# Second FFN's down product as seven half-size products, and softmax sums divided at the end of branch A

## Chip, cores and metric

One NeuronCore of a Trainium2 chip. The metric is the device time of one launch in microseconds: the median of three runs, and beside it one execution recorded by the profiler, from which all rows below come.

## Reference: what is computed

A decoder layer on 1024 tokens of width 1024 in fp32: a SwiGLU half-step, a token mixer of two causal attention branches, a second SwiGLU half-step. Each has an RMSNorm before and after. What the change touches:

```python
def swiglu(h, w_gate, w_up, w_down):                       # D_FF = 2816
    return (jax.nn.silu(h @ w_gate) * (h @ w_up)) @ w_down
...
    h = rms_norm(x, g_pre_ffn2[l]) * (1 + sc3) + sh3
    x = x + 0.5 * gt3 * rms_norm(swiglu(h, w_gate2[l], w_up2[l], w_down2[l]), g_post_ffn2[l])
...
# branch A, per block of 128 queries and each of 8 heads
    s = jnp.where(valid[:, :, None, :], s, -jnp.inf)
    p = jax.nn.softmax(s, axis=-1)
    return jnp.einsum('bqhk,bqkr->bqhr', p.astype(c_kv.dtype), ckv_sel)
```

## The kernel before

**Products.** Every large product is taken in three TensorE passes (`mm3`, L102): each fp32 operand is split into a high and a low part, high x high, low x high and high x low are summed in one PSUM bank. A split is one ScalarE cast (L76) and one VectorE subtraction (L77) of a 128x512 tile; `psplit` (L81, L82) puts the subtraction on GpSimd. The engines get their order from a planner in the framework (L1404, `schedule_with_timeline_sim=True`), so the order on an engine is not just that of the source; waits between engines are semaphores.

**Gate and up (`gate_up`, L252).** Both FFNs run gate and up already with seven half-size products in place of eight: for each of 11 blocks b of 256 hidden columns there are steps i = 0 to 6, each with 24 matmuls for gate and up (m = 0, 1). Sums of weight quarters are made by GpSimd (L286 to L289), sums of results by VectorE (L343, L346). In steps 1, 4, 5 and 6 one quarter of the activation is complete: ScalarE takes Silu (L349), GpSimd multiplies (L351), and a DMA of the SyncE queue (SP) stores the 256 KB to DRAM (L353). Step 1 gives the first token half and even hidden blocks, step 4 first half and odd, step 5 second half and odd, step 6 second half and even. The blocks b = 0 to 2 take steps 0 and 1 first ("early"). The result tile `p1` of step 1 has one buffer, `p0` three, `p2` and `p3` one each. Weights are prepared three steps ahead (LOOK, L27).

**Down (`down`, L368).** It loops three times over the 22 hidden chunks c: eight token tiles x first 512 columns, then token tiles 0 to 3 and 4 to 7 x the second 512 columns. For each chunk a 512 KB load of w_down feeds two chunks (L393), w_down and the activation are split, and each token tile gets three matmuls. The activation is read back from DRAM once (L389) into tiles that stay. Each finished bank is drained by ScalarE (sum of squares, L365) and VectorE (times the gain, L366). After the last chunk of a column half the kernel takes rsqrt of the sums and adds the residual (`post2`, L1363; DMAs L1366, L1369, L1379). In the last loop of the second FFN the last four chunks are kept back and run token tile by token tile, so that banks end one after another.

**Branch A (`branch_a`, L971).** 64 units (4 head pairs p, 2 heads e, 4 groups g, 2 blocks t). `scores`: three matmuls per 512 keys, then one VectorE instruction that masks, scales and takes the extreme (L1058), exp with the sum on ScalarE (L1061), reciprocal of the sum on VectorE (L1062), and GpSimd multiplies the probabilities with it (L1063). `mix`: TensorE transposes the probabilities (L1081), ScalarE and VectorE split them (L76, L77), TensorE multiplies with the values (L1091) after each second unit, ScalarE and VectorE add the two halves of the bank (L1095, L1097). With p = 2 each pair of units also carries a small combination of branch B (`combine_b`: VectorE on 4 to 12 elements per partition, L951 to L960; GpSimd L962 to L964).

Of the kernel before, what the change touches and what calls it, by code (L numbers as in the profile page):

```python
# [10 lines left out]
F32 = mybir.dt.float32  # L11
# [28 lines left out]
class Layer:  # L40
# [211 lines left out]
    def gate_up(self, W, raws, pools, V, wg, wu, actd):  # L252
# [64 lines left out]
        def steps(order, filler=None, ahead=()):  # L317
# [4 lines left out]
            for s, (b, i) in enumerate(order):  # L322
# [4 lines left out]
                for m in range(2):  # L327
# [19 lines left out]
                    if i in (1, 4, 5, 6):  # L347
                        if m == 0:
                            nc.scalar.activation(x[0], x[0], AF.Silu)  # L349
                        else:  # L350
                            nc.gpsimd.tensor_tensor(x[1], x[1], x[0], op=ALU.mult)  # L351
                            ff, h = {1: (0, 0), 4: (1, 0), 5: (1, 1), 6: (0, 1)}[i]
# [15 lines left out]
    def down(self, W, W2, wd, room, actd, y, G, junk, ss, post, filler=None):  # L368
# [6 lines left out]
        for dh, tiles in ((0, range(8)), (1, range(4)), (1, range(4, 8))):  # L375
# [3 lines left out]
            nlate = (1, LATE + (W2 is not None) * 2 if tiles[-1] == 7 else 1)[dh]  # L379
# [6 lines left out]
            for c in range(NF):  # L386
# [8 lines left out]
                pool = W2 if W2 is not None and nlate > 1 and NF - nlate <= c < NF - nlate + 2 else W  # L395
                w = [pool.tile([P, 512], F32R, name=f"d{n}", tag="w") for n in "hl"]
                self.split(w[0], w[1], r[:, c % 2])
                a = {}
                for h in halves:
                    a[h] = [pool.tile([P, 512], F32R, name=f"a{n}", tag="w") for n in "hl"]  # L400
# [21 lines left out]
        for _ in bg:  # L422
            pass
# [547 lines left out]
    def branch_a(self, aw, ap, late, G, mask, off):  # L971
# [73 lines left out]
        def scores(p, e, g, t):  # L1045
# [4 lines left out]
            st = late.tile([P, 2], F32, name="st", bufs=4)  # L1050
# [122 lines left out]
def layer_kernel(ctx, tc, aps, out):  # L1173
# [22 lines left out]
    with pool("w1", 12) as W, pool("g1") as wk, pool("r1", 5) as L.rawp:  # L1196
# [48 lines left out]
        with pool("f1a") as fa, pool("f1b") as fp:  # L1245
# [30 lines left out]
            L.down(W, None, aps["w_down1"], room, actd, y, A1, lambda: jkb, ss, post1, fill)  # L1276
# [31 lines left out]
    actd = L.dram.tile([DFF // P, P, S], F32, name="act2")  # L1308
    L.turns = {"pj": cycle(("pj", "s", "pj", "pt"))}
    with pool("w3", 13) as W, pool("r5", 3) as L.rawp, pool("o2") as op:  # L1310
# [36 lines left out]
        with pool("r6", 2) as r6, pool("vp2") as vp:  # L1347
# [60 lines left out]
```

## Time and profile before

| | us |
|---|---|
| median of 3 runs (lowest to highest) | 2521.93 (2517.61 to 2523.97) |
| the profiled execution, its own time | 2520.3 |
| its span in the profile | 2518.4 |
| TensorE busy (94% of the span) | 2357.4 |
| VectorE busy (64%) | 1611.1 |
| ScalarE busy (43%) | 1094.7 |
| GpSimd busy (38%) | 951.2 |
| DMA, mean over the span | 119 GB/s |
| TensorE clock granted, mean | 0.974 |

Busy shares are means over stages with different limits. Matmuls are pipelined in the records: the length of one record is not the time that it takes from the next, so TensorE's cost is read from the distance of starts. The stretches that matter are 1456 to 1646 us (branch A), 1900 to 2265 us (gate and up of the second FFN) and 2265 to 2518 us (its down product and the end).

### The profile page before, as it was taken

Reading aid. Unit: us, or ns where it says so; the run is one execution under the profiler, and the core shown is the slowest. Engines: PE = TensorE matmul, PEld = TensorE weight load, DVE = VectorE, ACT = ScalarE, POOL = GpSimd, SP = SyncE. Lnnn points to the kernel's source line nnn. Section 1 sums busy time; section 2 is a strip of 40 time slices with the busy share of each in tenths; the row PEclk is TensorE's granted clock in tenths of the full one; section 3 lists DMA queues with packets and bytes.
Section 4 is the critical chain, followed back from the end, with each engine's and each line's share of the span. In section 5 each row is a group of like instructions: output and inputs, shape, how many; then the busy total and the mean of one; then the engine's idle time right before and its main releaser. Section 6 shows DMA issues by size and latency. Waiting matters only on the chain.

```text
span 2518.4 us, 33990 instructions
## 1 busy us (share of the span) xinstructions
PE 2357.4 (94%) x11279; PEld 1978.4 (79%) x11279; DVE 1611.1 (64%) x3193; ACT 1094.7 (43%) x2342; POOL 951.2 (38%) x1109
## 2 busy tenths in 40 slices
PE   5799999999998999999989799899879999999997
PEld 4578887778787877889989677678658888888886
DVE  7866778754885145999963388874486554553455
ACT  5422322333454355777445466623443333333443
POOL 5675555400004433432243144601587454430012
PEclk9899999999998999999999799999989999999999
DMA  9234455761634233512421422154234323253134
GB/s 279 89 107 134 145 159 153 240 230 51 190 117 122 73 99 97 193 33 66 142 59 51 104 64 70 45 198 158 96 113 130 97 76 92 80 195 107 53 107 151
DMA packets 229804, 300.04 MB, mean 119 GB/s; under 512 B 23607, under 2 KB 144343, under 8 KB 229629
## 3 DMA queue, kind: packets, MB, share of 16 engines
q1 hardware_dynamic: 228988, 296.80, 37.4%
q8 instruction: 90, 1.47, 0.2%
q10 hardware_dynamic: 640, 1.07, 0.1%
q14 instruction: 86, 0.70, 0.1%
HBM read 233.98 MB, written 63.83 MB: 118 GB/s over the span
## 4 chain that ended last, share of the span: by engine, by line
PE 75%; DVE 11%; DMA 5%; issue 3%; ACT 3%; POOL 3%; SPq 0%; DVEq 0%; ACTq 0%; POOLq 0%
PE gu L104 9%; PE gu L105 9%; PE gu L106 9%; PE dn L105 6%; PE dn L106 6%; PE dn L104 6%; PE gpj L104 2%; PE gpj L105 2%; PE gpj L106 2%; PE bq L104 2%; DMA wr<-in_w_mod_dram 2%; PE bq L105 2%; PE bq L106 1%; PE apv L1091 1%; PE bv L104 1%
## 5 line engine op out<-in xcount | busy, mean ns | idle before, releaser
L104 PE MATMUL gu<-V,wh 128*128 128x512 f32 x1232 | 488.5, 397 | 18.9 <-ACT wh L76 9.3
L105 PE MATMUL gu<-V,wl 128*128 128x512 f32 x1232 | 487.3, 396 | 6.0 <-DVE wl L77 5.7
L106 PE MATMUL gu<-V,wh 128*128 128x512 f32 x1232 | 482.3, 394 | 4.5 <-DVE V L77 4.5
L77 DVE TENSOR_TENSOR wl<-rw,wh 128x512 fp32r<-128x512 f32 x232 | 214.1, 925 | 134.6 <-PE gu L105 93.7
L104 PEld LDWEIGHTS gu<-V,wh 128*128 128x128 f32 x1232 | 234.6, 191 | 73.3 <-ACT wh L76 11.3
L105 PEld LDWEIGHTS gu<-V,wl 128*128 128x128 f32 x1232 | 234.3, 190 | 59.7 <-DVE wl L77 8.9
L106 PEld LDWEIGHTS gu<-V,wh 128*128 128x128 f32 x1232 | 233.3, 190 | 56.5 <-DVE V L77 7.0
L105 PE MATMUL dn<-dh,al 128*128 128x512 f32 x704 | 275.6, 391 | 1.6 <-DVE al L77 1.6
L106 PE MATMUL dn<-dl,ah 128*128 128x512 f32 x704 | 274.4, 391 | 0.0
L104 PE MATMUL dn<-dh,ah 128*128 128x512 f32 x704 | 253.7, 391 | 6.0 <-DVE junk L197 6.0
L76 ACT CAST wh<-rw 128x512 fp32r<-128x512 f32 x232 | 140.1, 618 | 210.0 <-PE gu L106 126.3
L351 POOL TENSOR_TENSOR p<-p 128x512 f32<-128x512 f32 x86 | 129.9, 1511 | 247.3 <-DVE p L343 70.1
L343 DVE TENSOR_TENSOR p<-gu,p 128x512 f32<-128x512 f32 x252 | 170.0, 681 | 67.2 <-PE gu L106 35.6
L76 ACT CAST ah<-act 128x512 fp32r<-128x512 f32 x176 | 107.4, 621 | 182.3 <-PE dn L105 131.2
L77 DVE TENSOR_TENSOR al<-act,ah 128x512 fp32r<-128x512 f32 x176 | 118.0, 689 | 80.5 <-PE dn L105 42.5
L104 PEld LDWEIGHTS dn<-dh,ah 128*128 128x128 f32 x704 | 132.5, 188 | 33.9 <-DVE junk L197 6.4
L105 PEld LDWEIGHTS dn<-dh,al 128*128 128x128 f32 x704 | 132.7, 189 | 30.5 <-DVE al L77 3.2
L77 DVE TENSOR_TENSOR dl<-rd,dh 128x512 fp32r<-128x512 f32 x132 | 91.2, 692 | 101.4 <-PE dn L105 52.4
L106 PEld LDWEIGHTS dn<-dl,ah 128*128 128x128 f32 x704 | 132.9, 189 | 27.7
L349 ACT ACTIVATE p<-p 128x512 f32<-128x512 f32 x86 | 54.4, 633 | 215.4 <-DVE p L343 163.8
L185 DVE SCALAR_TENSOR_TENSOR macc<-wr,scol,macc 128x512 f32<-128x512 f32 x98 | 91.9, 938 | 56.0 <-DMA wr<-in_w_mod_dram 55.4
L76 ACT CAST dh<-rd 128x512 fp32r<-128x512 f32 x132 | 81.6, 618 | 83.3 <-PE dn L105 70.8
(465 smaller groups left out, 5465.4 us busy)
## 6 DMA issues: line engine op xcount, KB each, us to landing
rd<-in_w_down_dram SPq DMA_DIRECT2D x66, 512.0 KB
wr<-in_w_mod_dram SPq DMA_DIRECT2D x112, 256.0 KB
rw<-in_w_gate_dram SPq DMA_DIRECT2D x44, 512.0 KB
rw<-in_w_up_dram SPq DMA_DIRECT2D x44, 512.0 KB
act<-act SPq DMA_DIRECT2D x88, 256.0 KB
act<-p SPq DMA_DIRECT2D x86, 256.0 KB
wm<-in_w_mod_dram SPq DMA_DIRECT2D x32, 256.0 KB
x<-xt SPq DMA_DIRECT2D x16, 512.0 KB
```

The source lines that it names most:

```text
L76: self.nc.scalar.copy(hi, src)
L77: self.nc.vector.tensor_sub(lo, src, f(hi))
L104: mm(out, ah, bh, start=start, stop=False)
L105: mm(out, al, bh, start=False, stop=False)
L106: mm(out, ah, bl, start=False, stop=stop)
L185: nc.vector.scalar_tensor_tensor(acc, r, self.scol[:, k:k + 1], acc, op0=ALU.mult, op1=ALU.add)
L343: nc.vector.tensor_tensor(x[m], bk, y[m], op=ALU.add)
L349: nc.scalar.activation(x[0], x[0], AF.Silu)
L351: nc.gpsimd.tensor_tensor(x[1], x[1], x[0], op=ALU.mult)
L1091: nc.tensor.matmul(b[:, q0:256], VV[p][:, j, e, :], pt[j // 4][l][:, j % 4, q0:], start=j == 0 and l == 0, stop=j == nj - 1 and l == 1)
```

## The change

- **Down product.** `down7` replaces `down` in the second FFN (the first FFN keeps `down`, with the same loops). With the token halves and the even or odd hidden blocks as a 2x2 grid (a11, a12 second half of tokens; a21, a22 first half), and the same for w_down (b11 to b22), it takes seven products of 512 tokens x 1408 hidden x 512 columns: a11 b11, s3 (b22 - b12), s2 (b22 - b12 + b11), s1 (b12 - b11), a22 (b22 - b12 + b11 - b21), a12 b21, s4 b22, in this order.
- **Sums of w_down** are made by GpSimd just ahead of the split, for products 2 to 5, 11 chunks each; the running sum of products 2, 3 and 5 stays in two tiles `TT` and is updated in place, the sum of product 4 overwrites its load.
- **Sums of the activation** (s1 = a21 + a22, s2 = s1 - a11, s3 = a11 - a21, s4 = a12 - s2) are made in `gate_up` from the quarters while they are in SBUF: three on GpSimd, one on VectorE for each block b. Seven tiles per block go to DRAM instead of four (three early blocks also store a21 and read it back). `down7` reads one tile per chunk and product.
- **Buffers.** `down7` loads pairs of chunks: activation, w_down, and for products 2 and 4 a second part of w_down. Product 1 uses the buffers of `gate_up`; from product 2 the loads have six buffers of 512 KB (`dr2`), the splits 24 + 13 (`dw2`, `w3`). Two sets of four PSUM banks alternate. y and `TT` take the four large tiles.
- **Results** are summed in SBUF: VectorE adds each finished bank to one or two of the four quarters of y; a finished quarter gets its sum of squares (ScalarE, now from SBUF) and its gain (VectorE).
- **Branch A.** L1063 and the reciprocal per unit go. The sums of two units share a tile; after L1091 VectorE takes one reciprocal of 128x2, TensorE transposes it twice as a 128x128 broadcast into the free half of the bank, and VectorE multiplies the 64x256 result with it.

```diff
@@ gate_up
+        def operands(b, i, x):
+            out = lambda n, t: nc.sync.dma_start(ad[n, b], t)
+            sub = lambda E, o, x, y: E.tensor_tensor(o, x, y, op=ALU.subtract)
+            if i == 1:
+                tiles[b, "21"] = x
+                if b in early:
+                    out(7, x[1])
+                return
+            if i != 1:
+                tiles[b, {4: "22", 5: "12", 6: "11"}[i]] = x
+                out({4: 1, 5: 2, 6: 0}[i], x[1])
+            if i == 4:
+                if b in early:
+                    t = pools["p1"].tile([P, 2, 512], F32, name="p1", tag="p1", bufs=1)
+                    nc.sync.dma_start(t[:, 1], ad[7, b])
+                    tiles[b, "21"] = [t[:, 0], t[:, 1]]
+                nc.gpsimd.tensor_tensor(x[0], tiles[b, "21"][1], x[1], op=ALU.add)
+                out(3, x[0])
+            if i == 6:
+                (s1, _), (s3, a21), (s4, a12), (s2, a11) = (tiles[b, n] for n in ("22", "21", "12", "11"))
+                sub(nc.gpsimd, s2, s1, a11)
+                out(4, s2)
+                sub(nc.vector, s3, a11, a21)
+                out(5, s3)
+                sub(nc.gpsimd, s4, a12, s2)
+                out(6, s4)
...
+    def down7(self, Ws, raws, wd, T, ad, y, G, junk, ss, post, nlate):
...
+        tags = (("pj", "pj", "s", "pt"), ("tr", "tr", "o", "gg"))
...
+        def normed(r, c, t, E):
+            nc.scalar.activation(junk(), C(r, c, t), AF.Square, accum_out=sq(r, c, t))
+            E.tensor_tensor(C(r, c, t), C(r, c, t), G[:, dsl[c - 1]], op=ALU.mult)
...
+        def o6(b, t):
+            add(C(1, 2, t), C(1, 1, t), b)
+            add(C(2, 1, t), C(2, 1, t), b)
+
+        def o5(b, t):
+            add(C(1, 2, t), C(1, 2, t), b)
+            add(C(2, 2, t), C(2, 1, t), b)
+            normed(2, 2, t, nc.vector)
...
+        def o3(b, t):
+            add(C(1, 2, t), C(1, 2, t), b)
+            normed(1, 2, t, nc.vector)
...
+        prods = [(0, (b11,), o1), (5, (b22, SUB, b12, keep), o7), (4, (None, ADD, b11, keep), o6),
+                 (3, (b12, SUB, b11, not keep), o5), (1, (None, SUB, b21, keep), o4), (2, (b21,), o2), (6, (b22,), o3)]
+        bg = iter(())
+        for n, (A, B, end) in enumerate(prods):
+            bk = [self.bank("dn", tag=x) for x in tags[n % 2]]
+            nl = nlate if end is o3 else 1
...
+            for j in range(NB):
+                if j % 2 == 0:
+                    m = min(2, NB - j)
+                    ra = load(ad[A].rearrange("j p f -> p j f"), "ra", j, m)
+                    rb = load(B[0], "rd", j, m) if B[0] is not None else None
+                    if len(B) > 1:
+                        rc = load(B[2], "re", j, m)
+                        for k in range(m):
+                            o = T(j + k) if B[3] else rb[:, k]
+                            nc.gpsimd.tensor_tensor(o, o if B[0] is None else rb[:, k], rc[:, k], op=B[1])
+                w, a = ([Ws(n, j).tile([P, 512], F32R, name=f"{m}{x}", tag="w") for x in "hl"] for m in "da")
+                self.split(a[0], a[1], ra[:, j % 2])
+                self.split(w[0], w[1], T(j) if len(B) > 1 and B[3] else rb[:, j % 2])
+                if j >= NB - nl:
+                    late.append((j, w, a))
+                    continue
+                for t in range(4):
+                    mul(t, j, w, a)
+                if end in (o2, o3):
+                    next(bg, None)
...
+            for t in range(4):
+                for x in late:
+                    mul(t, *x)
+                end(bk[t], t)
+            if end is o4:
+                bg = post(0)
+        for _ in post(1):
+            pass
@@ branch_a
-            nc.scalar.activation(Pm, Pm, AF.Exp, bias=mx[:, nb - 1:nb], scale=-1.0, accum_out=st[:, 1:2])
-            nc.vector.reciprocal(st[:, 1:2], st[:, 1:2])
-            nc.gpsimd.tensor_tensor(Pm, Pm, st[:, 1:2].to_broadcast([P, n]), op=ALU.mult)
+            nc.scalar.activation(Pm, Pm, AF.Exp, bias=mx[:, nb - 1:nb], scale=-1.0,
+                                 accum_out=state["st"][:, t % 2:t % 2 + 1])
...
+            st = state["st"]
+            nc.vector.reciprocal(st, st)
+            for x in range(2):
+                nc.tensor.transpose(b[:, 256 + x * P:256 + (x + 1) * P], st[:, x:x + 1].to_broadcast([P, P]), self.ident)
             tmp = late.tile([P, 256], F32, name="otmp", bufs=2)
             nc.scalar.copy(tmp[main, :], b[oth, :256])
             od = of[g // 2][main, (g % 2) * 256:(g % 2 + 1) * 256]
             nc.vector.tensor_add(od, b[main, :256], tmp[main, :])
+            nc.vector.tensor_mul(od, od, b[main, 256:512])
```

## Rows read from the trace of the kernel before

**Rows 1.** Windows: us from:to, length, busy (count) per engine, PEclk, DMA share, GB/s
```profile
1960.00:2260.00 300.00, 300.00 (x1325) 248.44 (x1325) 153.62 (x204) 95.42 (x158) 134.07 (x103) 1.00 0.33 104
...
2265.50:2385.90 120.40, 120.40 (x533) 99.72 (x532) 47.30 (x72) 42.62 (x78) 1.29 (x1) 1.00 0.25 85
...
2446.00:2506.60 60.60, 59.44 (x261) 48.54 (x259) 34.38 (x54) 24.40 (x47) 19.56 (x45) 1.00 0.40 136
```

**Rows 2.** Timeline, TensorE in the down stage: start, length, instruction
```profile
2265.58 0.39 PE L104 MATMUL dn<-dh,ah 128*128 128x512 f32 x1
...
2371.66 0.39 PE L104 MATMUL dn<-dh,ah 128*128 128x512 f32 x1
...
2374.38 0.39 PE L104 MATMUL dn<-dh,ah 128*128 128x512 f32 x1
...
2506.20 0.39 PE L106 MATMUL dn<-dl,ah 128*128 128x512 f32 x1
```

**Rows 3.** Groups by line, 2300 to 2500 us: count, busy us, mean ns, idle before
```profile
L77 DVE TENSOR_TENSOR al<-act,ah 128x512 fp32r<-128x512 f32 x72 | 48.2, 687 | 30.6 <-PE dn L105 30.6
L76 ACT CAST ah<-act 128x512 fp32r<-128x512 f32 x72 | 44.9, 625 | 108.0 <-PE dn L105 80.9 <-PE dn L106 27.0
...
L366 DVE TENSOR_TENSOR y<-dn,G 128x512 f32<-128x512 f32 x13 | 8.8, 689 | 6.6 <-ACT junk L365 6.5
```

**Rows 4.** Groups by line, 1900 to 2265 us (gate and up)
```profile
L77 DVE TENSOR_TENSOR wl<-rw,wh 128x512 fp32r<-128x512 f32 x112 | 107.4, 960 | 123.2 <-PE gu L105 93.0 <-issue 11.7 <-ACT p L349 7.2
...
L343 DVE TENSOR_TENSOR p<-gu,p 128x512 f32<-128x512 f32 x120 | 81.6, 682 | 39.1 <-PE gu L106 16.2 <-POOL p L351 13.1 <-POOL wl L82 5.7
```

**Rows 5.** Timeline, VectorE beside GpSimd, in branch A and in gate and up
```profile
1547.17 0.73 DVE L1058 CUSTOM_DVE_ANT_0 aP<-as,mask,mx 128x512 f32<-128x512 f32 x1
...
1547.83 1.27 DVE L952 TENSOR_TENSOR cM<-cM,br 128x4 f32<-128x4 f32 x1
...
1547.39 1.68 POOL L1063 TENSOR_TENSOR aP<-aP,st 128x896 f32<-128x896 f32 x1 [6.70 <-DVE st L1062]
...
2262.91 1.27 DVE L77 TENSOR_TENSOR al<-act,ah 128x512 fp32r<-128x512 f32 x1 [0.80 <-PE gu L105]
...
2262.34 1.29 POOL L351 TENSOR_TENSOR p<-p 128x512 f32<-128x512 f32 x1 [4.88 <-DVE p L346]
```

**Rows 6.** Timeline, VectorE where the first column half ends
```profile
2380.48 0.68 DVE L77 TENSOR_TENSOR dl<-rd,dh 128x512 fp32r<-128x512 f32 x1
...
2381.56 1.41 DVE L366 TENSOR_TENSOR y<-dn,G 128x512 f32<-128x512 f32 x2 [0.40 <-ACT junk L365]
```

**Rows 7.** DMA view of 2230 to 2290 us, GB/s in 40 slices of 1.5 us
```profile
GB/s 96 254 218 371 384 403 399 385 386 389 385 391 404 366 214 214 0 216 235 178 255 403 395 250 249 393 366 363 388 401 395 343 251 11 0 0 0 35 310 15
```

**Rows 8.** Chain that ended last: start, us, what
```profile
1470.80 0.45 PE apt L1081 x4
...
2507.77 3.56 DMA xt<-x
```

**Rows 9.** Windows of branch A and one ahead of it (columns of rows 1)
```profile
1400.00:1420.00 20.00, 7.75 (x46) 6.47 (x45) 5.91 (x16) 8.12 (x20) 6.77 (x8) 0.64 0.64 150
...
1490.00:1540.00 50.00, 48.69 (x318) 41.74 (x318) 42.37 (x127) 38.19 (x94) 21.77 (x20) 1.00 0.26 74
1540.00:1580.00 40.00, 34.30 (x209) 29.12 (x208) 35.96 (x109) 24.89 (x60) 20.38 (x18) 0.91 0.23 68
1580.00:1620.00 40.00, 29.59 (x183) 24.48 (x181) 36.05 (x107) 24.52 (x64) 26.96 (x26) 0.96 0.21 61
```

**Rows 10.** Groups by line, 1460 to 1650 us (branch A)
```profile
L1063 POOL TENSOR_TENSOR aP<-aP,st 128x896 f32<-128x896 f32 (+3 forms) x64 | 74.2, 1171 | 109.6 <-DVE st L1062 103.3 <-PE apt L1081 3.4 <-DVE ce L960 1.5
...
L1097 DVE TENSOR_TENSOR of<-apv,otmp 64x256 f32<-64x256 f32 x32 | 13.4, 419 | 2.4 <-ACT otmp L1095 1.8
L1062 DVE RECIPROCAL st<-st 128x1 f32<-128x1 f32 x63 | 9.6, 154 | 3.2 <-ACT aP L1061 2.9
...
L952 DVE TENSOR_TENSOR cM<-cM,br 128x4 f32<-128x4 f32 x8 | 6.8, 846 | 0.0
```

More of the change, by code (lines that the diff above doesn't have):

```diff
@@ L351, in steps @@
                             nc.gpsimd.tensor_tensor(x[1], x[1], x[0], op=ALU.mult)
+                            if ad is not None:
+                                operands(b, i, x)
+                                continue
                             ff, h = {1: (0, 0), 4: (1, 0), 5: (1, 1), 6: (0, 1)}[i]
@@ L366, in evac, with down @@
         self.nc.vector.tensor_tensor(y, b, g, op=ALU.mult)
-    def down(self, W, W2, wd, room, actd, y, G, junk, ss, post, filler=None):
+    def down(self, W, wd, room, actd, y, G, junk, ss, post, filler=None):
         nc = self.nc
@@ L378, in down @@
             late, last = [], dh == 1
-            nlate = (1, LATE + (W2 is not None) * 2 if tiles[-1] == 7 else 1)[dh]
+            nlate = LATE if dh and tiles[-1] == 7 else 1
             def mul(t, c, w, a):
@@ L394, in down @@
                                       .rearrange("(k p) f -> p k f", p=P))
-                pool = W2 if W2 is not None and nlate > 1 and NF - nlate <= c < NF - nlate + 2 else W
-                w = [pool.tile([P, 512], F32R, name=f"d{n}", tag="w") for n in "hl"]
+                w = [W.tile([P, 512], F32R, name=f"d{n}", tag="w") for n in "hl"]
                 self.split(w[0], w[1], r[:, c % 2])
@@ L399, in down @@
                 for h in halves:
-                    a[h] = [pool.tile([P, 512], F32R, name=f"a{n}", tag="w") for n in "hl"]
+                    a[h] = [W.tile([P, 512], F32R, name=f"a{n}", tag="w") for n in "hl"]
                     self.split(a[h][0], a[h][1], room[c][h])
@@ L1049, in scores @@
             mx = late.tile([P, 2], F32, name="mx", bufs=4)
-            st = late.tile([P, 2], F32, name="st", bufs=4)
+            if t == 2 * g:
+                state["st"] = late.tile([P, 2], F32, name="st", bufs=4)
             nb = (n + 511) // 512
@@ L1274, in post1 @@
                         yield
-            L.down(W, None, aps["w_down1"], room, actd, y, A1, lambda: jkb, ss, post1, fill)
+            L.down(W, aps["w_down1"], room, actd, y, A1, lambda: jkb, ss, post1, fill)
     off, o = {}, 0
@@ L1307, in layer_kernel @@
     x2 = L.dram.tile([S, D], F32, name="x2")
-    actd = L.dram.tile([DFF // P, P, S], F32, name="act2")
+    ad = L.dram.tile([8, NB, P, 512], F32, name="act2")
     L.turns = {"pj": cycle(("pj", "s", "pj", "pt"))}
@@ L1346, in layer_kernel @@
         L.turns = gu_turns()
-        with pool("r6", 2) as r6, pool("vp2") as vp:
+        r6x = ExitStack()
+        r6 = r6x.enter_context(pool("r6", 2))
+        with pool("vp2") as vp:
             r5 = L.rawp
             GU = L.gate_up(W, cycle((r5, r5, r5, r6, r6)), {"p0": op, "p1": op, "p2": op, "p3": vp, "s": vp}, V,
-                           aps["w_gate2"], aps["w_up2"], actd)
+                           aps["w_gate2"], aps["w_up2"], ad=ad)
             L.second_half(V, ys, sh, lambda i: bigv(i) if i == 4 else
@@ L1355, in layer_kernel @@
             L.turns = {}
-        with pool("w4", 8) as W2, pool("f2") as fp:
-            room = rooms((fp, fp))
-            y = [fp.tile([P, 4, D], F32, name=f"y{h}") for h in range(2)]
+        with r6x, pool("dr2", 6) as dr, pool("dw2", 24) as dw:
+            y = [L.big.tile([P, 4, D], F32, name=f"y{h}", tag="big") for h in range(2)]
+            TT = [L.big.tile([P, 8, 512], F32, name="TT", tag="big") for _ in range(2)]
             G3 = op.tile([P, D], F32, name="G3", tag="p1")
@@ L1380, in post2 @@
                     yield
-            L.down(W, W2, aps["w_down2"], room, actd, y, G3, lambda: jk, ss, post2)
+            r56 = cycle((r5, r5, r5, r6, r6))
+            Ws = lambda n, j: W if n == 0 or j % 3 == 2 else dw
+            raws = lambda n, j: next(r56) if n == 0 else dr
+            L.down7(Ws, raws, aps["w_down2"], lambda j: TT[j // 8][:, j % 8], ad, y, G3, lambda: jk, ss, post2, 4)
 _INS = ["x", "c", "positions", "w_mod", "b_mod", "g_pre_ffn1", "w_gate1", "w_up1", "w_down1", "g_post_ffn1",
```

32 lines of the change are left out of this document (31 added, 1 removed).

## Prediction, worked out step by step

> **What bounds the kernel now.** I read the page's busy shares first and then did not use them: TensorE's 94% is a mean over stages. The table by stage comes next [rows 1]: in gate and up of the second FFN TensorE is busy 300.00 of 300.00 us at a granted clock of 1.00, and in the first column half of the down product 120.40 of 120.40 us, while VectorE is busy for 47.30, ScalarE for 42.62 and DMA for 0.25 of it. So both stages of the second FFN end when TensorE has done its count of matmuls, and what shortens them is fewer matmuls. The third view is the timeline, for the price of one. A record lasts 0.39 us, but that is not the price: the first matmul for one chunk and token half starts at 2371.66, the one twelve later at 2374.38 [rows 2], so twelve cost 2.72 us and one costs 0.2267 us. The stage runs from 2265.58 to the end of its last record, 2506.20 + 0.39 = 2506.59 [rows 2]: 241.0 us for 1056 matmuls, 1.6 us more than 1056 x 0.2267 = 239.4. Branch A is the other kind of stage: in 1540 to 1580 us VectorE is busy 35.96 and TensorE 34.30 of 40 us, and 1580 to 1620 is worse for TensorE (29.59) with VectorE at 36.05; in 1490 to 1540, TensorE has 48.69 of 50 [rows 9]. There the two engines wait for each other, with TensorE ahead early on and VectorE later.
>
> **Down product: the matmuls.** Seven products of 11 chunks x 4 token tiles x 3 passes are 924 matmuls in place of 1056. 132 x 0.2267 = 29.9 us less, all on the path, since TensorE has no idle time in that stage. The form of a matmul (128x128 by 128x512) stays. This term has one answer if TensorE stays fed, so the rest of the part asks who feeds it. One product lasts 132 x 0.2267 = 29.9 us, one pair of chunks 5.44 us.
>
> **Down product: splits, sums, drains.** The count of splits stays at 154 (7 x 11 x 2 against 66 + 44 + 44). A split costs ScalarE 0.625 and VectorE 0.687 us [rows 3], so a product costs VectorE 22 x 0.687 = 15.1 us of 29.9. Added are 44 sums on GpSimd, 11 in each of products 2 to 5. A GpSimd operation on 128x512 takes 1.29 us [rows 5], so 14.2 us per product. GpSimd alone has room for that, but the two engines shut each other out: at 1547.83 VectorE starts on a 128x4 operation and needs 1.27 us, to 1549.10, while GpSimd's multiplication runs from 1547.39 to 1549.07; the operation just ahead, which reads PSUM, needed only 0.73 us beside the same multiplication, and a split beside GpSimd took 1.27 us from 2262.91, where GpSimd ran until 2263.63 [rows 5]. Where both inputs lie in SBUF the two engines take turns. In gate and up, with GpSimd busy 134.07 of 300 us [rows 1], the mean split is 0.960 us and the sum from PSUM stays at 0.682 [rows 4]. At 0.960, a product with sums costs VectorE 21.1 us. Drains grow: 32 additions from PSUM at 0.682 and 16 gains at 0.689 [rows 3], up to 8 and 4 at one product's end (8.2 us after the fourth product). The dearest product then has VectorE at 21.1 + 8.2 = 29.3 of 29.9 us. That is just enough, and there is a lead: 37 split buffers hold nine chunks of four, 9 x 2.72 = 24.5 us. Drains sit in VectorE's queue, but the planner does put splits of the next part among them: at 2380.48 a split for the next column half runs ahead of the first drain at 2381.56 [rows 6].
>
> The Trainium skill (SBUF — State Buffer, section "SBUF: two separate sides") speaks against this change in one point: it calls the port pair of VectorE and GpSimd an exclusive lock held for the whole instruction, and "the other fully blocks". The two rows at 1547 us agree to 0.03 us. By the softer mean of gate and up the stage keeps its 29.9 us; by the lock at its hardest it loses the price of the first rival below.
>
> **Down product: loads.** A pair brings 1.0 MB, in products 2 and 4 1.57 MB in 5.44 us, so 290 GB/s. With the same rows of 2 KB the DMA view shows slices of 385 to 404 GB/s [rows 7], so 1.57 MB moves in about 4.0 us. A lone 512 KB load lands after 3.56 us [rows 8], about 2.2 us of it ahead of the bytes (an estimate: 3.56 less 0.52 MB at 390 GB/s). Six buffers hold two pairs of three loads: 4.0 + 2.2 to land, then two sums (2.6 us) and the last splits (about 1.4): 10.2 us for a slot, 5.1 us per pair with two slots, against 5.44 needed. If splits and sums take strict turns (4 x 0.687 + 2.6 = 5.4 after landing) it is 5.8 us per pair, 0.4 x 5.5 pairs x 2 products = 4 us, out of a lead of up to 24.5. I take 2 us for the stage's stalls in all, between 0 and 14. The start has one answer: product 1 uses buffers that gate and up leaves one by one, and before, too, splits for the down product ran during the last steps of gate and up (the one at 2262.91 [rows 5]), so the first matmul followed at once; if that cover went, the first load and split would show, 3.56 + 0.63 + 0.69 = 4.9 us.
>
> **Gate and up.** Per block (168 matmuls, 38.1 us) GpSimd gets three operations more (3.9 us), VectorE one (0.7), DMA three stores. TensorE has 300.00 of 300.00 there with GpSimd busy for 45% and VectorE for 51% [rows 1], so they become some 55% and 53%. One new wait: the tile `p1` (one buffer) now lives from step 1 to the landing of s3 after step 6. After the last matmul come 0.68 (sum), 1.29 (product), 0.69 (s3), and a store on the SP queue behind s2's, about 3.6 us at most: 6.3 us. It is needed at the first drain of the next block's step 1, 36 matmuls or 8.2 us later. Behind that addition VectorE's splits would queue, which are three steps (16 us) ahead. I take 0, with +4 as the far end, and nothing below zero since TensorE has no gap to give.
>
> **The end.** The last bank's drain gains one addition (0.68 us) ahead of its square sum, on the path; the chain through the third buffer of xt (3.56 us, [rows 8]) is as before. +0.7, from 0 to +2.
>
> **Branch A.** Removed: 64 GpSimd multiplications, 74.2 us of its time, and 64 reciprocals of 0.154 us, 9.9 us of VectorE [rows 10]. Added on VectorE: 32 reciprocals (4.9) and 32 multiplications of 64x256 from PSUM, nearest to the addition of the same shape there at 0.419 us (13.4). On TensorE: 64 transposes; four take 0.45 us [rows 8], so 7.2 us. Net, VectorE gets +8.4 us. What it gets back is the shut-out: L952 takes 0.846 us for four elements where 0.154 would do, 5.5 us over eight, and five like lines beside it lose on a smaller scale; GpSimd keeps L962 to L964, so I count about twice L952's loss, 12 us, all with p = 2, in 1540 to 1620. And each unit's chain from exp to transposes loses 0.15 + 1.17 us. In the first half TensorE is the bound and pays half of its transposes, +3.6 us. In 1540 to 1620 TensorE sat idle for 5.70 + 10.41 = 16.1 us [rows 9]; half of that, 8 us, I count as won, and 0.4 us as lost for the bank that L1091 writes (held 0.42 + 0.2 us longer, at the few groups that wait for it). -8 + 3.6 + 0.4 = -4, between -14 (all of the idle time but 2) and +7 (only the transposes).
>
> **The sum.** From the profiled execution's 2520.3 (2518.4 of span and 1.9 around it): -29.9 +2 +0 +0.7 -4 = -31.2, so 2489.1. The median of the three runs is 2521.93, 1.6 above the profiled one; I stay at 2489.
>
> **Rivals.**
> 1. Sums and splits exclude each other fully and the lead is small. Four products then cost VectorE and GpSimd together 11 x (2 x 0.687 + 1.29) = 29.3 us each, plus drains that don't overlap (0, 2.7, 5.5, 8.2): 133.6 against 119.6 us. With no lead, +14 in place of +2: 2501. For: the rows at 1547. Against: drains read PSUM and don't exclude; the lead. 18%.
> 2. Branch A gains all that TensorE idles: -14 in place of -4, 2479. For: VectorE at 36 of 40 us there. Against: chains through ScalarE stay. 12%.
> 3. Slower: at each of six product borders the drains stand ahead of the next splits, so no lead ever builds. TensorE then waits at each border for two drains (1.4), a sum (1.3) and a split (1.3), 4 us, 24 in all; the 14 us of rival 1 come in full; and after such waits the granted clock falls as in 1400 to 1420, where TensorE was busy 7.75 of 20 us and had 0.64 [rows 9]: some 3 us at the lower level (1.2 GHz) after each border cost 1.5 us each, 9 in all. 47 us against 29.9, 4 for branch A: 2520.3 - 29.9 - 4 + 0.7 + 47 = 2534. It decides once stalls pass 41 us. Against: [rows 6]. 5%.
> 4. The change does not do what it says: the stalls eat about 30 us and the time stays, 2515 to 2525. 4%.
>
> **How the numbers follow.** Forecast, 2481 to 2498: 61%, at 2489. The range of 80% takes in rival 1 and most of rival 2: 2478 to 2506. About 0.3% (7.6 us) is what a measurement of this kernel can tell from no change, so faster means below 2514.4: forecast, rivals 1 and 2 (91%) less a tail of 1: 0.90. Same 0.05, slower 0.05.
>
> **What would show it.** In the changed profile: 924 matmuls on `dn` of the second FFN, first to last about 211 us; TensorE at 1.00 in all 20 us windows of it; VectorE's splits at 0.9 to 1.1 us in products 2 to 5 and 0.69 elsewhere; gate and up still without TensorE idle; branch A some 4 us shorter, with L952 near 0.15 us. Wrong would make it: TensorE waiting for splits or GpSimd sums at product borders, a load rate that ends below 290 GB/s in products 2 and 4, or clock below 1.00 there.

## The result, and the profile after

The changed kernel takes 2492.23 us (median of four runs, 2484.66 to 2496.68) where the kernel before takes 2519.77 on the same chip: a ratio of 0.9885, 95% interval 0.9868 to 0.9903. The profiled execution took 2492.64 us, with a span of 2490.9. Both spans, cut at the same instructions:

| stretch | before, us | after, us | difference | in the prediction's sum |
|---|---|---|---|---|
| start to the first `gu` matmul of the second FFN | 1816.7 | 1812.0 | -4.7 | -4 |
| gate and up, to the first `dn` | 448.9 | 448.8 | -0.1 | 0 |
| down stage, first `dn` to the end of the last | 241.0 | 215.3 | -25.7 | -29.9 + 2 |
| from there to the end | 11.8 | 14.8 | +3.0 | +0.7 |
| span | 2518.4 | 2490.9 | -27.5 | -31.2 |

Windows of the changed kernel, with the columns of [rows 1]: gate and up, then the down stage in seven pieces of 29.92 us, about one product each.

```profile
1960.80:2260.80 300.00, 300.00 (x1326) 248.40 (x1325) 170.21 (x213) 94.82 (x157) 181.13 (x128) 1.00 0.35 114
...
2260.80:2290.72 29.92, 29.92 (x133) 24.56 (x131) 15.53 (x21) 10.50 (x20) 9.90 (x7) 1.00 0.79 282
2290.72:2320.64 29.92, 27.95 (x124) 23.04 (x124) 17.32 (x23) 15.78 (x30) 13.42 (x10) 1.00 0.76 255
2320.64:2350.56 29.92, 29.92 (x134) 24.78 (x133) 25.00 (x29) 12.82 (x23) 18.75 (x13) 1.00 0.64 211
2350.56:2380.48 29.92, 29.92 (x134) 24.77 (x133) 18.13 (x30) 11.37 (x21) 12.05 (x10) 1.00 0.76 266
2380.48:2410.40 29.92, 28.16 (x122) 22.38 (x121) 29.46 (x33) 13.30 (x29) 14.31 (x9) 1.00 0.61 187
2410.40:2440.32 29.92, 29.92 (x134) 24.77 (x133) 19.61 (x30) 15.53 (x33) 13.63 (x31) 1.00 0.60 206
2440.32:2470.24 29.92, 29.82 (x131) 23.97 (x130) 22.14 (x36) 12.82 (x28) 3.58 (x6) 1.00 0.61 229
```

Gate and up is full on TensorE with GpSimd at 60% in place of 45%. In the down stage TensorE is full in four pieces; it lacks 1.97 us in the second and 1.76 us in the fifth, where VectorE is busy 29.46 of 29.92 us. The clock is 1.00 throughout. TensorE's timeline names the gaps (start, length, instruction, in brackets its idle time before and what ended it):

```profile
2260.77 0.39 PE L104 MATMUL dn<-dh,ah 128*128 128x512 f32 x1
...
2292.82 0.50 PE L104 MATMUL dn<-dh,ah 128*128 128x512 f32 x1 [1.97 <-ACT dh L76]
...
2392.31 0.50 PE L106 MATMUL dn<-dl,ah 128*128 128x512 f32 x1 [0.82 <-DVE dl L77]
2403.74 0.50 PE L104 MATMUL dn<-dh,ah 128*128 128x512 f32 x1 [0.71 <-ACT dh L76]
2404.71 0.50 PE L106 MATMUL dn<-dl,ah 128*128 128x512 f32 x1 [0.23 <-DVE dl L77]
...
2475.65 0.39 PE L106 MATMUL dn<-dl,ah 128*128 128x512 f32 x1
```

924 matmuls at the 0.2267 us of [rows 2] are 209.5 us; the stage is 5.8 us over that, 3.7 of it in these four gaps. Read from the distances of starts, which also count the slow matmuls right behind a gap, product 2 loses 2.2 us, product 5 2.6 and product 7 0.6. The first gap lies where ScalarE's queue holds the four drains of product 1 ahead of the second product's first cast. ScalarE's timeline there:

```profile
2290.21 2.05 ACT L476 COPY y<-dn 128x512 f32<-128x512 f32 x4 [2.07 <-PE dn L106]
2292.12 0.65 ACT L76 CAST dh<-TT 128x512 fp32r<-128x512 f32 x1
```

The other gaps lie in product 5. Ahead of the first of them VectorE's splits and GpSimd's sums run side by side; VectorE's rows stand first:

```profile
2379.68 2.38 DVE L77 TENSOR_TENSOR al<-ra,ah 128x512 fp32r<-128x512 f32 x2
2381.99 3.48 DVE L77 TENSOR_TENSOR dl<-TT,dh 128x512 fp32r<-128x512 f32 x2
2385.39 1.77 DVE L77 TENSOR_TENSOR al<-ra,ah 128x512 fp32r<-128x512 f32 x1
...
2379.93 10.09 POOL L530 TENSOR_TENSOR TT<-TT,re 128x512 f32<-128x512 f32 x6 [0.71 <-DMA re<-in_w_down_dram]
```

Six sums take 10.09 us, 1.68 each, and the splits beside them go at the same pace: from 2380.29 on one split and one sum start every 1.70 us. The drains of product 4 come only after that gap, and the next two gaps stand behind them: VectorE has eight additions and four gains to do, and ScalarE, which had waited 8 us for a load of the activation, has square sums between its casts:

```profile
2397.38 1.27 DVE L469 TENSOR_TENSOR y<-y,dn 128x512 f32<-128x512 f32 x2
...
2401.42 1.14 ACT L76 CAST ah<-ra 128x512 fp32r<-128x512 f32 x2 [8.01 <-DMA ra<-act]
2402.46 0.63 ACT L472 ACTIVATE junk<-y 128x512 bf16<-128x512 f32 x1
```

By the groups of the whole stage (count, busy us, mean ns):

```profile
L77 DVE TENSOR_TENSOR al<-ra,ah 128x512 fp32r<-128x512 f32 x74 | 61.8, 845 | 20.2 <-ACT ah L76 15.9 <-PE dn L105 3.6 <-issue 0.5
...
L530 POOL TENSOR_TENSOR TT<-TT,re 128x512 f32<-128x512 f32 x22 | 35.0, 1616 | 12.0 <-DMA re<-in_w_down_dram 8.8 <-DVE dl L77 1.8 <-DVE y L469 1.3
L77 DVE TENSOR_TENSOR dl<-TT,dh 128x512 fp32r<-128x512 f32 x33 | 32.1, 981 | 15.3 <-ACT dh L76 15.0
...
L469 DVE TENSOR_TENSOR y<-y,dn 128x512 f32<-128x512 f32 x31 | 19.8, 677 | 1.1 <-PE dn L106 1.1
```

Both engines are slower than alone (0.687 us in [rows 3], 1.29 in [rows 5]), while the drains, which read PSUM, keep 0.677 (0.672 to 0.687, ten of them beside a sum).

The tail grew for a reason that stands in VectorE's queue:

```profile
2474.82 0.68 DVE L469 TENSOR_TENSOR y<-y,dn 128x512 f32<-128x512 f32 x1
2477.42 1.41 DVE L1513 SCALAR_TENSOR_TENSOR xt<-y,sums,xt 128x512 f32<-128x512 f32 x2 [1.92 <-POOL sums L95]
...
2479.35 0.68 DVE L469 TENSOR_TENSOR y<-y,dn 128x512 f32<-128x512 f32 x1
...
2485.76 1.42 DVE L1513 SCALAR_TENSOR_TENSOR xt<-y,sums,xt 128x512 f32<-128x512 f32 x2
```

TensorE's last record ends at 2476.04, yet the last bank's addition starts at 2479.35: the residual of the second tile is queued ahead of it and waits 1.92 us for GpSimd's rsqrt. In the kernel before the queue had the same order and the last drain began 2.1 us after TensorE, but ScalarE didn't wait for it with the square sum, which it took from the bank, 0.1 us after TensorE's end at 2506.59:

```profile
2506.69 0.60 ACT L365 ACTIVATE junk<-dn 128x512 bf16<-128x512 f32 x1 [2.03 <-PE dn L106]
```

Now the square sum reads what the addition writes, and starts only at 2480.12.

In branch A the groups that answer to [rows 10]: the new multiplications and reciprocals on VectorE, and L1080, which was L952:

```profile
L1231 DVE TENSOR_TENSOR of<-of,apv 64x256 f32<-64x256 f32 x31 | 12.9, 415 | 0.7
...
L1224 DVE RECIPROCAL st<-st 128x2 f32<-128x2 f32 x32 | 5.0, 156 | 1.9 <-ACT aP L1190 1.8
...
L1080 DVE TENSOR_TENSOR cM<-cM,br 128x4 f32<-128x4 f32 x8 | 1.2, 150 | 0.0
```

From the first score matmul to the end of the last `apv` the stretch is 7.6 us shorter (199.6 to 192.0). At the first matmul of the output projection (`wo`) 3.8 us of that are left, since the up projection in between now waits:

```profile
PE upa L104 <- DVE gab L1278: 3.5, 1, 3.5
```

VectorE in turn waits there for the gates, `gab<-gd` by DMA. Before, TensorE's longest wait in that stretch was 1.6 us. What moved is the order in the SyncE queue. Before, the first load of the gates stands ahead of the second load of weights for the up projection (`wubr`), which waits until VectorE has split the first one:

```profile
1642.23 0.34 SPq L1133 DMA_DIRECT2D gab<-gd  x1
...
1649.42 0.38 SPq L506 DMA_DIRECT2D wubr<-in_w_up_b_dram  x1
```

In the changed kernel it stands behind it, and starts 3.2 us after the last `apv` in place of 3.7 us ahead of it:

```profile
1639.92 0.37 SPq L634 DMA_DIRECT2D wubr<-in_w_up_b_dram  x1
1640.39 0.41 SPq L1267 DMA_DIRECT2D gab<-gd  x1
```

### The profile page after: what moved, and what is told of

Read it like the earlier page. It is cut to its first block, busy times and chain, and to the rows that moved or that the text cites. A ratio compares the mean times of both kernels' runs of the same rounds, so it can differ in the third digit from the quotient of the medians.

```text
span 2490.9 us, 33864 instructions
## 1 busy us (share of the span) xinstructions
PE 2333.2 (94%) x11211; PEld 1956.6 (79%) x11211; DVE 1664.0 (67%) x3236; ACT 1091.1 (44%) x2346; POOL 1002.8 (40%) x1122
## 4 chain that ended last, share of the span: by engine, by line
PE 69%; DVE 14%; DMA 7%; issue 4%; POOL 4%; ACT 3%; SPq 0%; DVEq 0%; POOLq 0%; ACTq 0%
PE gu L105 9%; PE gu L104 9%; PE gu L106 9%; PE dn L106 4%; PE dn L105 4%; PE dn L104 4%; PE gpj L104 2%; DMA wr<-in_w_mod_dram 2%; PE gpj L105 2%; PE gpj L106 2%; PE bq L104 2%; PE bq L105 2%; PE bq L106 1%; DMA re<-in_w_down_dram 1%; DVE wl L77 1%
## 5 line engine op out<-in xcount | busy, mean ns | idle before, releaser
L105 PE MATMUL dn<-dh,al 128*128 128x512 f32 x660 | 256.9, 392 | 0.2 <-DVE al L77 0.2
L106 PE MATMUL dn<-dl,ah 128*128 128x512 f32 x660 | 255.2, 392 | 1.1 <-DVE dl L77 1.0
L104 PE MATMUL dn<-dh,ah 128*128 128x512 f32 x660 | 239.0, 392 | 9.1 <-DVE junk L197 6.4
L104 PEld LDWEIGHTS dn<-dh,ah 128*128 128x128 f32 x660 | 124.3, 189 | 35.9 <-DVE junk L197 6.8
L106 PEld LDWEIGHTS dn<-dl,ah 128*128 128x128 f32 x660 | 124.6, 189 | 28.4 <-DVE dl L77 2.7
L105 PEld LDWEIGHTS dn<-dh,al 128*128 128x128 f32 x660 | 124.5, 189 | 27.3 <-DVE al L77 1.3
L76 ACT CAST dh<-rd 128x512 fp32r<-128x512 f32 x110 | 67.9, 619 | 117.5 <-PE dn L105 75.6
L77 DVE TENSOR_TENSOR dl<-rd,dh 128x512 fp32r<-128x512 f32 x110 | 77.1, 704 | 52.2 <-ACT dh L76 48.9
L104 PE MATMUL gpj<-uh,gw 128*128 128x512 f32 x256 | 103.8, 406 | 7.5 <-ACT gt L910 7.3
L849 DVE TENSOR_SCALAR_CACHE_REDUCE mask<-isc,cand 128x384 bf16<-128x384 f32 (+1 forms) x124 | 108.7, 877 | 2.6
```

The lines of the kernel that those rows point to most:

```text
L76: self.nc.scalar.copy(hi, src)
L77: self.nc.vector.tensor_sub(lo, src, f(hi))
L104: mm(out, ah, bh, start=start, stop=False)
L105: mm(out, al, bh, start=False, stop=False)
L106: mm(out, ah, bl, start=False, stop=stop)
L849: nc.vector.tensor_scalar(mask[:, :(t + 1) * P], sc[t], 0.0 if v is None else one(f(v), t), 0.0, op0=op, op1=ALU.add, accum_out=one(cnt, t))
```

## Experiments

Theory A: the gain is the removed matmuls, and what is missing in the down stage is lost where GpSimd's sums slow the splits. Theory B: the loads come late. Theory C: drains stand in the queues ahead of the next product. Stage lengths are first `dn` to the end of the last, from the profile of each kernel; in the changed kernel and four others whose code for this stage is the same it is 215.3 to 217.2 us, so 1 us more or less says little. Branch A (first score matmul to the end of the last `apv`) takes 189.4 to 193.8 us in the changed kernel and the six others with the same code for it, so 2 us there say little. The experiments on the down stage alone, `e5_o1` to `e8_one_load`, are one execution each.

**The two halves alone.** `e1_branch_a` is the kernel before with the new `branch_a`; `e2_down7` the changed kernel with the old one.

> The kernel before with the edit of branch A alone. By the prediction's step this is worth 4 us: the first matmul of the output projection (`wo`) moves from 1710.8 to about 1706 us, the end from 2518.4 to about 2514 us, and the down stage of the second FFN keeps its 241.0 us. Rival: in the changed kernel the first 4.8 us came from another order that the planner found because of the other edits; then this kernel stays within 1 us of before. Second rival: branch A alone gains more (to 14 us) and the rest of the changed kernel gave some of it back.

> The changed kernel with the old branch A, so the seven products alone. By the prediction's steps: 29.9 us less in the down stage, stalls of 2 us, 0.7 us at the end: 27 us under the kernel before. By what the changed kernel's trace shows (the down stage 215.3 us long, the tail 3.0 us longer): 22.7 us under it. If the two edits help each other, it is less than 20 us; if they are independent, this and the kernel with branch A's edit alone add up to the changed kernel's gain of 27.5 us within 2 us.

Branch A alone: ratio 0.9977 (0.9967 to 0.9987), 2513.35 against 2520.48 us; first `wo` at 1703.3, the down stage 241.0 us. That is more than the prediction's 4 us, and from the first score matmul to `wo` this kernel gains 8.3 us where the changed one gains 3.8, with the same code: the kernels with this code for both stages lie between 256.3 and 260.8 us there. The products alone: 0.9911 (0.9890 to 0.9933), 2496.60 us; stage 216.2, tail 14.7 us. The parts add up, 7.1 + 23.9 = 31.0 against 27.5 us, within the intervals. So nothing shows that the two edits help or hinder each other, and the rival that the early gain came from elsewhere falls.

**Sums on VectorE** (`e6_sum_vector`), **no sums** (`e7_no_sum`), **one load less** (`e8_one_load`).

```diff
# e6
-nc.gpsimd.tensor_tensor(o, o if B[0] is None else rb[:, k], rc[:, k], op=B[1])
+nc.vector.tensor_tensor(o, o if B[0] is None else rb[:, k], rc[:, k], op=B[1])
# e7: the sums go, the splits read a load
-self.split(w[0], w[1], T(j) if len(B) > 1 and B[3] else rb[:, j % 2])
+self.split(w[0], w[1], (rc if rb is None else rb)[:, j % 2])
# e8
-rc = load(B[2], "re", j, m)
+rc = load(B[2], "re", j, m) if rb is None else rb
```

> The changed kernel with the 44 sums of w_down on VectorE in place of GpSimd. If GpSimd's sums shut VectorE out for their whole length (1.4 to 1.6 us for a sum that VectorE does in about 0.69 us), then VectorE with the sums as its own work (22 splits x 0.687 + 11 x 0.687 = 22.7 us a product, with drains 22.7 to 30.9 us of 29.9) is no worse off: the stage stays at 215.3 us or falls to 212 us. If the two engines share most of the time, VectorE becomes the bound from the fourth product on and the stage grows to 218 us or more. If the gaps have nothing to do with the sums, 215 us.

> The changed kernel with all loads of the down stage but without the 44 sums: the splits of products 2 to 5 read one loaded tile, so these products use wrong w_down operands. If the sums beside the splits make the gaps where the fifth product begins (0.82 + 0.71 + 0.23 us, VectorE busy 29.54 of 30.0), these gaps go, splits take 0.69 us throughout, and the stage falls from 215.3 to about 212.5 us, with the 2 us at the second product's start left. Rival: loads and drains make the gaps; then the stage stays within 1 us of 215.3.

> The changed kernel without the second load of w_down in the products 2 and 4 (the sum reads the first tile twice, so these two products use wrong operands); sums, splits and drains as they are. If the loads of these products (1.57 MB a pair through six buffers, rates of 282, 255, 211, 265, 188 GB/s in products 1 to 5) hold the lead down, TensorE's gaps at the borders into products 3 and 5 fall, and the stage is 1 to 3 us shorter than 215.3 us. Rival: buffers are freed by VectorE's splits, so loads are late because VectorE is, and the stage stays within 0.5 us.

Without sums the stage is 209.6 us long and has no gap: the 924 matmuls at their price. Its first and last matmul:

```profile
2263.61 0.39 PE L104 MATMUL dn<-dh,ah 128*128 128x512 f32 x1
...
2472.82 0.39 PE L106 MATMUL dn<-dl,ah 128*128 128x512 f32 x1
```

With the sums on VectorE it is 212.2 us, with one gap left, the 1.97 us behind ScalarE. Groups of that kernel's stage:

```profile
L77 DVE TENSOR_TENSOR al<-ra,ah 128x512 fp32r<-128x512 f32 x74 | 49.9, 685 | 15.8 <-ACT ah L76 12.7 <-PE dn L105 2.9
...
L530 DVE TENSOR_TENSOR TT<-TT,re 128x512 f32<-128x512 f32 x22 | 14.3, 684 | 2.0 <-DMA re<-in_w_down_dram 2.0
```

Every split is back at 0.685 us. One window of each kernel from the first `dn` to the end of the last (columns of rows 1, VectorE third), first the changed kernel, then the sums on VectorE, then no sums:

```profile
2260.77:2476.04 215.27, 211.43 (x925) 172.77 (x923) 150.66 (x204) 93.30 (x181) 90.24 (x96) 1.00 0.67 229
...
2259.95:2472.12 212.17, 210.19 (x925) 173.13 (x923) 154.16 (x248) 93.39 (x181) 26.21 (x51) 1.00 0.66 232
...
2263.61:2473.21 209.60, 209.60 (x925) 173.23 (x923) 129.45 (x204) 94.72 (x181) 26.25 (x51) 1.00 0.67 235
```

As its own work the 44 sums add 24.7 us to VectorE's busy time; done by GpSimd, in 64.0 us of its time, they still add 21.2. So handing them over saved VectorE 3.5 us in all. With one load less, the splits stay slow (1.09 us for `dl<-TT`) and the stage is 211.9 us, again with the gap of 2 us behind ScalarE alone (the sums of product 4, which read one tile twice there, are also shorter, 1.16 us for 1.30). So at the fifth product neither the slow splits nor the loads make a gap by themselves in these runs; the lead carries one of them and not both. Theories A and B both hold there, as two halves of one cause. With GpSimd, product 2 moved 255 GB/s; with the sums on VectorE and the same loads, 320 GB/s (after 282 and 246 in product 1): DMA had more to give. From 2290 to 2320 us in the changed kernel the load queue waited 11.5 us for splits and 11.2 us for sums to free a buffer.

**Product 1's drains on VectorE** (`e5_o1`): `nc.scalar.copy(C(1, 1, t), b)` becomes `nc.vector.tensor_copy(C(1, 1, t), b)`.

> The changed kernel with the four drains of the first product as copies on VectorE in place of ScalarE. Theory: TensorE's longest gap in the down stage, 1.97 us where the second product begins, comes from ScalarE's queue, in which the four copies (2290.21 to 2292.2 us) stand ahead of the next product's first casts; on VectorE, busy 17.28 of 29.9 us there, the copies leave the casts free, the gap falls under 0.5 us and the stage from 215.3 to about 213.3 us. Rival: the copies then stand ahead of the next splits' second half on VectorE (four at 0.68 us, 2.7 us), and the gap stays at 1.5 to 2.7 us.

The gap behind ScalarE is gone, and gaps of 0.67, 0.26 and 0.99 us behind VectorE appear in products 2 and 3:

```profile
2290.27 0.96 PE L106 MATMUL dn<-dl,ah 128*128 128x512 f32 x3 [0.67 <-DVE dl L77]
...
2334.51 0.50 PE L106 MATMUL dn<-dl,ah 128*128 128x512 f32 x1 [0.99 <-DVE dl L77]
```

The stage is 214.3 us, 1 to 3 us less than with ScalarE. Theory C is right for the place (in the kernel without sums the casts run ahead of the copies, and there is no gap), but most of the gap comes back behind the engine that takes the copies.

**The tail** (`e4_tail`): the rsqrt of token tiles 4 to 6 on VectorE as well.

```diff
-L.rsqrt(s1[:, 2:3], s1[:, 0:1], 1, 1.0 / D, "r" if t < 7 else "p", nc.gpsimd if t < 7 else nc.vector)
+L.rsqrt(s1[:, 2:3], s1[:, 0:1], 1, 1.0 / D, "p", nc.vector)
```

> The changed kernel with the last four token tiles' rsqrt chains all on VectorE in place of three on GpSimd. Theory: the tail behind TensorE's last matmul is 14.8 us, not 11.8, since VectorE's queue holds `xt<-y,sums,xt` of the second tile ahead of the last bank's addition and waits 1.92 us there for GpSimd's second chain; with no wait for GpSimd the tail falls to 11.5 to 13 us and the whole by 2 to 3 us. Rival: the tail is longer by VectorE's own work (one addition more for each bank, 2.7 us); then four chains on VectorE (some 1.9 us each) leave the tail at 14.8 us or make it longer.

The tail is 12.9 us. VectorE's queue in it:

```profile
2476.64 0.68 DVE L469 TENSOR_TENSOR y<-y,dn 128x512 f32<-128x512 f32 x1
...
2484.11 1.41 DVE L1513 SCALAR_TENSOR_TENSOR xt<-y,sums,xt 128x512 f32<-128x512 f32 x2 [0.33 <-DVE sums L95]
```

The last addition starts 0.35 us after TensorE's end, and 1.9 of the 3.0 us come back. The remaining 1.1 is about the prediction's term. The whole kernel is at 2489.19 us, ratio 0.9876 (0.9856 to 0.9896), which doesn't set it apart from the changed kernel's 0.9885.

**What branch A's division costs.** `e3_no_division` leaves out reciprocals, transposes and multiplications; `e13_mult_only` keeps the multiplications alone (`tensor_mul(od, od, b[main, :256])`).

> The changed kernel with branch A's division left out altogether: no reciprocals (5.0 us of VectorE), no 64 transposes of the sums, no 32 multiplications (13.3 us of VectorE), so what branch A hands on is not divided. It tells what the new division costs on the path. The prediction charged 3.6 us for transposes where TensorE is the bound, 0.4 us for the held bank, and let VectorE's added 8.4 us stand against what it won: if that is right, the first `wo` comes 4 to 9 us earlier than in the changed kernel (1706.0 us), with 4 us from TensorE and the rest from VectorE. Rival: the division is hidden beside other waits; then within 1.5 us of the changed kernel. Other rival: VectorE is the bound in all of the second half; then 10 us or more.

> The changed kernel with the 32 multiplications of branch A kept (by the bank's own left half, the same shape from PSUM), and without the reciprocals and the 64 transposes; so branch A is not divided. From the first score matmul to the last `apv` the changed kernel takes 192.0 us, with neither transposes nor multiplications 176.5 us, with a quarter of VectorE's work for it and half of the transposes 186.5 us. If the transposes make the cost (TensorE's own time, and the bank held until they are read), this takes 177 to 181 us. If VectorE's 13.3 us of multiplications do, 184 to 190 us. In between, both do in parts.

Without any division the kernel takes 2471.63 us, some 20 us less than the changed one (its `wo` comes 20.0 us earlier after the first score matmul): more than the first theory allowed (4 to 9), and in size the last rival of its text. The gates' loads stand ahead of that of `wubr` here, as before the change, and TensorE waits for them for 0.5 us, though branch A is at its shortest. With the multiplications alone branch A takes 191.4 us, so the multiplications cost nearly all, and what reciprocals and transposes cost is less than the spread. The kernel as a whole takes 2496.70 us: TensorE waits 6.5 us for the gates, the output projection is 1.9 us longer at a granted clock of 0.92, and behind the 1.97 us gap of product 2 the granted clock is 0.50, the lower of its two levels (1.2 GHz), from 2295.9 to 2299.1 us, so that matmuls start every 0.43 us. One window of each kernel, from the first score matmul to the end of the last `apv` (columns of rows 1: length, TensorE, weight loads, VectorE, ...); the kernel before:

```profile
1446.27:1645.90 199.63, 175.14 (x1091) 148.65 (x1091) 169.69 (x501) 131.26 (x320) 102.53 (x92) 0.96 0.22 64
```

the changed kernel:

```profile
1445.23:1637.20 191.97, 175.76 (x1155) 151.36 (x1155) 160.72 (x500) 129.93 (x320) 29.26 (x28) 0.98 0.23 67
```

branch A's edit alone (`e1_branch_a`):

```profile
1447.02:1636.40 189.38, 173.29 (x1155) 148.47 (x1155) 161.16 (x500) 129.71 (x320) 29.25 (x28) 1.00 0.23 68
```

no division:

```profile
1441.34:1617.80 176.46, 168.41 (x1091) 143.05 (x1091) 145.65 (x437) 130.00 (x320) 28.72 (x28) 1.00 0.25 72
```

multiplications alone:

```profile
1442.11:1633.49 191.38, 172.05 (x1092) 144.66 (x1093) 161.38 (x469) 131.41 (x321) 29.07 (x28) 0.98 0.23 67
```

Length less VectorE's busy time is 29.9, 31.3, 28.2, 30.8 and 30.0 us. TensorE is busier than VectorE in each, and still the length follows VectorE one for one, to some 3 us. The multiplications also hold the bank that the next `apv` needs; in the changed kernel TensorE's waits that a VectorE instruction ended come to some 13 us there, and 3.0 of them are for that bank, so it is the smaller part.

**A cheaper division** (`e9_late_div`): once per head pair and token half. The reciprocals of 4 blocks x 2 heads are spread by one ScalarE copy, transposed four times into a bank of tag `gg`, and one 128x512 multiplication takes the place of four of 64x256.

```diff
+nc.vector.reciprocal(st, st)                    # 128x8
+nc.scalar.copy(wide, st.unsqueeze(3).to_broadcast([P, 4, 2, 64]))
+bd = self.bank("odv", tag="gg")
+for x in range(4):
+    nc.tensor.transpose(bd[:, x * P:(x + 1) * P], wide[:, x].rearrange("p e c -> p (e c)"), self.ident)
...
+nc.vector.tensor_mul(of[h], of[h], bd)
```

> The changed kernel with branch A's division once per pair of heads and half of the tokens: 32 transposes in place of 64, 8 multiplications of 128x512 (about 0.68 us each, 5.4 us) in place of 32 of 64x256 (13.3 us), 8 reciprocals in place of 32, and 8 copies of 0.6 us more on ScalarE that spread the reciprocals. Theory: the kernel without any division gave 20 us back, 7.4 us of them TensorE's own and the rest idle time of TensorE, which follows VectorE's 18.3 us; here half of TensorE's part and 12 us of VectorE's go, so the first `wo` comes 10 to 13 us earlier than in the changed kernel (after 260.8 us from the first score matmul, so 248 to 251 us). Rival: what costs is the chain at each group's end (bank held by transposes, copy, addition, multiplication) rather than the load of the engines; then nearly all 20 us come back, 243 us or less. Other rival: ScalarE's added copies and the bank that keys and combines share take the place of it, 256 us or more.

From the first score matmul to `wo` 256.7 us: the last case of the text, against 260.8 in the changed kernel. Branch A itself fell to 187.0 us:

```profile
1442.01:1629.05 187.04, 172.14 (x1123) 147.08 (x1123) 153.35 (x452) 135.41 (x328) 28.30 (x28) 0.99 0.23 69
```

VectorE has 7.4 us less than in the changed kernel, not 12, and the length followed by 4.9. Length less VectorE is 33.7 here, the most of all; the keys' last matmul, whose bank the division now shares, came 111 us after the first score matmul in place of 89. Past branch A 0.9 us go to the up projection, where TensorE waits 3.0 us for `gab` again, and 4.0 more by the first `dn`, with a granted clock of 0.92 in place of 0.95 in the output projection; why it was lower stays open. The kernel takes 2489.98 us, 0.9884 (0.9869 to 0.9899): no better in the sum.

**All together.** `e11_combo`: late division, sums on VectorE, product 1's drains on VectorE, four rsqrt chains on VectorE. `e12_combo`: the same with chains 1 and 3 on GpSimd.

> The late division, the sums of w_down on VectorE, the first product's drains on VectorE and all four last rsqrt chains on VectorE, together. If the parts add up: 10 to 13 us from branch A, 3.1 us from the sums, up to 2 us from the drains (the stage at 210 to 212 us), 2 us in the tail: 17 to 20 us under the changed kernel, 2472 to 2475 us. If VectorE with sums and copies is too full in the second product (25.1 + 2.7 of 29.9 us), the stage stays at 212 to 214 us.

> As the kernel before it in this list, with two of the last four rsqrt chains on GpSimd (the first and the third) and two on VectorE. If in the tail the wait is for GpSimd, its tail is up to 2 us longer than with all on VectorE; if it is VectorE's own load (four chains of 1.9 us ahead of the last bank's addition, which started at 2476.64, 0.35 us after TensorE's end), it is up to 2 us shorter than 12.9 us.

2483.65 us, ratio 0.9860 (0.9844 to 0.9877), and 2483.80 us, 0.9857 (0.9842 to 0.9871). Both are some 8 us under the changed kernel by their medians, half of what the first text added up, with intervals that still touch its 0.9868 to 0.9903. The stage is 213.0 us in both, with gaps of 1.41 and 1.38 us in product 2: VectorE takes sums and copies in turn there, and ScalarE's first cast waits 3.46 us for a sum (`e11_combo`), as the text's last sentence had it. The tails are 12.2 and 13.4 us; in the second one VectorE waits 1.23 us for GpSimd once more, so the wait is what counts and not VectorE's own load.

## Why the prediction was right, and where its terms were off

- **The bound and the 29.9 us.** Right: TensorE's count of matmuls sets the stage. 924 matmuls in 209.6 us, where nothing holds them up, are the 0.2267 us of [rows 2].
- **Stalls in the down stage, +2.** The stage fell by 25.7 and not by 27.9, so the added stalls are 4.2 us, inside the bounds of 0 to 14 and twice the value taken. Two causes were each named and each thought covered. Splits and sums did take turns, 1.70 us a pair. The lead carried that except in product 5: its first gap comes ahead of the drains of product 4, the other two behind them and behind a late load. The drains ahead of the next product's work came too (rival 3's mechanism), most of all at one of six borders and on ScalarE, which the prediction didn't ask about: product 1 alone drains there.
- **The mean split of 0.960 us**, taken from gate and up [rows 4], was near: 0.845 for the activation and 0.981 for `TT`. By starts, splits alone follow each other every 0.60 us (`e7_no_sum`) and sums alone every 1.25, 1.85 us together, and a pair takes 1.70. The lock that the Trainium skill states for the two engines (SBUF — State Buffer, section "SBUF: two separate sides"), by which one waits out the other's whole instruction, agrees with that to 0.15 us.
- **Loads.** 255 and 266 GB/s in products 2 and 4, below the 290 that the prediction named as a sign of failure, at little harm (product 2's loads had partly come during product 1, at 282 GB/s). The cause is the buffers' release, as the 10.2 us per slot had it, and not DMA.
- **Gate and up, 0.** Right: 448.8 for 448.9 us, GpSimd at 60% (some 55 expected), VectorE at 57% (53).
- **The end, +0.7 from 0 to +2.** Wrong, +3.0. The sum counted the added operation, 0.68 us, and not its place: the square sum, which had passed VectorE's queue by reading the bank, now stands behind that queue and its wait for GpSimd. `e4_tail` empties the queue and gives 1.9 us back. This is the term that failed.
- **Branch A, -4.** The sum was met (-4.7 at the second FFN, -3.8 of it between the first score matmul and `wo`) by luck, through terms that were not; kernels with the same code gained up to 8.3 us there. VectorE got back 18.1 us on the six combine lines (28.4 to 10.3 us over eight calls; L952 from 846 to 150 ns) and not 12. Each microsecond of VectorE counts whole and not half: 9.0 us less of it, 7.6 us less of length. The transposes were charged at 3.6 us; with the reciprocals they cost less than the runs can tell. And 3.9 of the 7.6 us went in the next stage, most of it in the wait for the gates, a step that the sum lacked.
- **Rivals.** 1 (no lead) didn't come: of the four products with sums TensorE ran full in two, and in a third it lost to ScalarE's queue and not to the turns. 2 was right that the idle time is there to be had (24.5 us before, 8.1 without a division); the new multiplications take most of it. 3's drains held TensorE up at one border of six for 2 us in place of 4, and the clock stayed at 1.00 in the changed kernel; in `e13_mult_only` it was 0.50 for 3.2 us behind the same gap and cost some 1.6 us, and the other kernels with this gap kept 1.00. 4 did not come.

## What to carry to other kernels

Before work is handed from VectorE to GpSimd, ask whether VectorE's neighbours in time read both inputs from SBUF: here 44 sums on GpSimd relieved VectorE of 3.5 us of 24.7, and the stage was 3 us shorter with the sums on VectorE. In a stretch where no engine is full, compare its length with each engine's busy time over several variants: what the length follows one for one is what to cut, here VectorE at 84% and not TensorE at 92%. After an edit, look at what now stands in a queue ahead of a step that used to pass it: a load that waits for a buffer ahead of the next stage's loads, a residual that waits for a scale ahead of the last drain. The two took back some 6 us here.

## What the runs showed that was not expected

VectorE and GpSimd, each with both inputs in SBUF, lengthened each other: splits from 0.685 to 0.845 and 0.981 us, sums from 1.29 to 1.62 us, a pair 1.70 us. Among the instructions of four to twelve elements in branch A the worst took 0.85 us beside GpSimd and 0.15 without it; the 18.1 us that the six of them gave back are more than the whole 9.0 us by which VectorE's busy time fell, as the new division took some 8. The granted clock of the output projection was 0.95 in the changed kernel, 0.92 with the late division and 0.97 without any; the runs don't say why.
